# Layer norm with a residual: groups of two rows, whole 2 MB loads to the end, and fifteen tiny reads on the lowest DMA engines

## The chip, the cores and the metric

The kernel runs on one core of a Trainium2 chip. The metric is the time on the device in microseconds (us), a median over several executions. All executions used here were at a granted clock of 1.0. The profiled execution has a *span* of its own, about 2 us shorter than its measured time; times of day inside an execution count from the start of that span. ACT, DVE and POOL are the scalar, vector and GpSimd engines; the sync queue (SPq) computes nothing here, it issues DMAs. A *landing* is the semaphore update with which one DMA engine reports that its share of a DMA is done.

## The reference

```python
# x, residual: (16, 1024, 512) float32; gamma = 1, beta = 0, eps = 1e-5
z = x + residual
mean = np.mean(z, axis=-1, keepdims=True)
var = np.var(z, axis=-1, keepdims=True)
return gamma * (z - mean) / np.sqrt(var + eps) + beta
```

There are 16,384 rows of 512 numbers. Each of the 128 partitions takes 128 of them, so "a row" below is one row in every partition: 128 x 512 numbers, 256 KB. Two inputs are read and one output is written: 67.11 MB in, 33.55 MB out. Nothing can be left out of that.

## The kernel before

```python
X_CHUNKS = [8] * 15 + [4, 4]          # rows for each load of x
R_CHUNKS = [8] * 15 + [4, 4]          # ... of the residual
OUT_CHUNKS = [16] * 7 + [8, 4, 4]     # ... for each store
GROUP = 4                             # rows for each step of the computation
Z_ROWS = 64                           # ring of x; the result is written in place
R_ROWS = 32                           # ring of the residual
STORE_LAG = 40
...
def add(g):                           # POOL: one instruction a group
    nc.gpsimd.tensor_tensor(out=z, in0=z, in1=part(rbuf, R_ROWS, j0, n), op=ALU.add)

def statistics(g):                    # ACT
    for k in range(n):                # minus the mean of each row
        nc.scalar.activation(out=junk, in_=zrow(j0 + k), func=ACT.Identity,
                             scale=-inv_d, accum_out=nm[:, k : k + 1])
    for k in range(n):                # sum of squares of each row
        nc.scalar.activation(out=junk, in_=zrow(j0 + k), func=ACT.Square,
                             bias=nm[:, k : k + 1], accum_out=ssq[:, k : k + 1])
    nc.scalar.activation(out=std[:, :n], in_=ssq[:, :n], func=ACT.Sqrt,
                         bias=eps_t[:, 0:1], scale=inv_d)      # one a group
# DVE: affine1 (z + nm) * gamma, row by row; reciprocal of std, one a group;
#      affine2 z * rstd + beta, row by row
...
for lo, n in spans(X_CHUNKS):         # everything is issued from the one sync queue
    asked = lo + n
    load_x(lo, n)
    while loads_r and loads_r[0][0] + loads_r[0][1] <= asked:
        while added < loads_r[0][0] + loads_r[0][1] - R_ROWS:
            added, done = next(steps) # add, statistics, affine1, affine2 of a group
        load_r(*loads_r.pop(0))
    ...
    store_due()                       # stores of all rows up to asked - STORE_LAG
```

A load of x waits until the store of the rows that lay in the same place of the ring has landed. When the last load has been issued, 48 rows (12 MB) are left whose stores are not yet issued.

## Time and profile before

| | before |
|---|---|
| time, median | 243.29 us (243.09 to 243.51) |
| span of the profiled execution | 241.3 us |
| busy: ACT, DVE, POOL | 180.1, 178.5, 144.3 us |
| moved by DMA | 100.67 MB |
| last store issued | 225.3 us |

First the head of the profile page: the busy time of each engine; then the DMA engines' busy share in tenths and GB/s, in 40 slices of 6 us; then the DMA queues.

```profile
span 241.3 us, 1109 instructions
## 1 busy us (share of the span) xinstructions
PE 4.1 (2%) x4; PEld 1.0 (0%) x4; DVE 178.5 (74%) x290; ACT 180.1 (75%) x546; POOL 144.3 (60%) x36
...
DMA  7999999999999999999999999999999999999992
GB/s 261 434 435 434 434 430 418 421 425 432 432 470 436 391 426 421 429 434 426 430 434 437 430 424 429 429 451 410 425 426 432 475 387 418 462 434 432 413 410 117
...
## 3 DMA queue, kind: packets, MB, share of 16 engines
q1 hardware_dynamic: 6336, 100.67, 97.9%
q14 instruction: 9, 0.07, 0.1%
...
```

DMA is at nine tenths or more from the second slice to the second last. No compute engine is busy for more than 75% of the span. Queue q1 carries the kernel's loads and stores; q14 carries nine packets of kind "instruction".

The stretches of the span, with the DMA share and GB/s at the end of each line:

```profile
...
core 0: us, PE busy (x) PEld busy (x) DVE busy (x) ACT busy (x) POOL busy (x), PEclk, DMA share, GB/s
13.00:82.00 69.00, 0.00 (x0) 0.00 (x0) 60.69 (x99) 64.14 (x196) 63.05 (x14) 1.00 1.01 429
82.00:205.00 123.00, 0.00 (x0) 0.00 (x0) 99.82 (x162) 99.95 (x305) 71.98 (x16) 1.00 1.00 429
205.00:225.00 20.00, 0.00 (x0) 0.00 (x0) 17.83 (x29) 14.55 (x45) 9.05 (x2) 1.00 1.03 440
225.00:235.00 10.00, 0.00 (x0) 0.00 (x0) 0.00 (x0) 0.00 (x0) 0.00 (x0) 1.00 0.96 411
235.00:241.30 6.30, 0.00 (x0) 0.00 (x0) 0.00 (x0) 0.00 (x0) 0.00 (x0) 1.00 0.31 133
...
```

(DMA shares of 1.01 and 1.03 show that a short stretch is good to a few per cent only.) 429 GB/s is all there is: in the packet records of the trace a 16 KB packet takes 0.611 us, so 16 engines together move at most 16 x 16,384 B / 0.611 us = 429 GB/s. 100.67 MB take 234.7 us at that rate. Averaged over the 16 engines, the records show 2.0 us without a packet of the kernel's queue in the first 10 us (none starts before 1.7) and about 0.2 us in all the time from 10 to 230 us; that is what the nine packets of q14 take (9 x 0.309 us / 16).

What is lost beside the start is lost at the end. A DMA of 128 partitions is split over 16 engines, and the trace holds the moment at which each engine's share has landed. For the last store (us from the start of the span, sorted):

```
before: 236.83 236.88 236.91 236.96 236.97 236.98 236.99 237.07 237.12 237.13
        237.17 237.24 237.40 238.03 | 240.04 240.15
```

(The prediction below has these times 0.04 us later: it counted them from a slightly different start.) Two engines land about 3 us after the median of the 16. At 30 us they were not late. How they fall behind shows when their landing is set against the median of the 16 for one DMA after the other, beside the starts of q14's 8 KB packets:

```
before, the latest two of 16, us behind the median
landing near:   32    37    52    57    71    82    111   115   140   174   206   218   237
second latest: 0.11  0.11  0.10  0.58  0.56  0.79  0.98  1.47  1.71  2.24  2.18  2.92  2.95
latest:        0.11  0.60  0.59  0.89  1.08  0.83  1.11  1.98  1.98  2.56  2.52  3.03  3.05
8 KB packets of q14 at: 33.0, 52.6, 77.8, 115.0, 134.6, 169.2, 195.0, 217.4, 218.2
```

After nearly every packet of the instruction queue (not after that at 195.0) one of the two is 0.3 to 0.7 us later. A 16 KB packet that started at 33.3 us, as the first such packet ended, took 0.986 us instead of 0.611; that both ran on one engine is inferred, since the records don't name the engine of a packet.

Groups of instructions of the profile page that the change touches (busy us, mean ns of one | idle before them):

```profile
...
L120 POOL TENSOR_TENSOR zbuf<-zbuf,rbuf 128x2048 f32<-128x2048 f32 x32 | 144.1, 4526 | 70.6 <-DMA rbuf<-in_residual_dram 69.6
...
L148 ACT ACTIVATE std<-ssq,eps_t 128x4 f32<-128x4 f32 x32 | 8.5, 267 | 1.0
L173 DVE RECIPROCAL rstd<-std 128x4 f32<-128x4 f32 x32 | 5.6, 175 | 0.0
...
```

What the sync queue waited for (us in total, times, longest), and its last instructions. L84 issues the loads of x, L87 those of the residual, L90 the stores. The last line says that the fifth store from the end was issued at 181.26 and that the last one was over 44.08 us later, at 225.34.

```profile
...
engine line waited for: us in total, times, longest us
SPq L84 <- DMA out_dram<-zbuf: 112.2, 4, 29.9
...
```

```profile
...
176.36 0.33 SPq L87 DMA_DIRECT2D rbuf<-in_residual_dram  x1
181.26 44.08 SPq L90 DMA_DIRECT2D out_dram<-zbuf  x5
```

### The profile page before, as it was taken

What the parts mean: (1) busy time and instruction counts of PE and PEld (TensorE: products, weight loads), DVE (VectorE), ACT (ScalarE), POOL (GpSimd) and SP (SyncE); (2) the same over time, 40 slices, a digit from 0 to 9 for tenths busy, and PEclk for the clock granted to TensorE, in tenths of its full rate; (3) what the DMA queues carried; (4) which work ended last, traced back from release to release, by engine and by line L of the source; (5) the groups of instructions that cost most, each with busy time, mean ns of one, the idle gap of its engine ahead of it and who ended that gap; (6) DMA issues with size and microseconds to landing.
All of it is one profiled execution on the core that took longest, in us unless ns stands there. A gap on an engine that the chain in (4) does not pass through costs nothing.

```text
span 241.3 us, 1109 instructions
## 1 busy us (share of the span) xinstructions
PE 4.1 (2%) x4; PEld 1.0 (0%) x4; DVE 178.5 (74%) x290; ACT 180.1 (75%) x546; POOL 144.3 (60%) x36
## 2 busy tenths in 40 slices
PE   3300000000000000000000000000000000000000
PEld 0000000000000000000000000000000000000000
DVE  0005999999999999899934999359991699969200
ACT  2009999999999999999709997099961999697000
POOL 0088988989889507894078940889209891860000
DMA  7999999999999999999999999999999999999992
GB/s 261 434 435 434 434 430 418 421 425 432 432 470 436 391 426 421 429 434 426 430 434 437 430 424 429 429 451 410 425 426 432 475 387 418 462 434 432 413 410 117
DMA packets 6349, 100.74 MB, mean 417 GB/s; under 512 B 706, under 2 KB 706, under 8 KB 708
## 3 DMA queue, kind: packets, MB, share of 16 engines
q1 hardware_dynamic: 6336, 100.67, 97.9%
q14 instruction: 9, 0.07, 0.1%
q10 hardware_dynamic: 4, 0.00, 0.0%
HBM read 67.11 MB, written 33.55 MB: 417 GB/s over the span
## 4 chain that ended last, share of the span: by engine, by line
DMA 62%; ACT 16%; DVE 6%; POOL 6%; SPq 1%; issue 1%; DVEq 0%; POOLq 0%
DMA rbuf<-in_residual_dram 34%; DMA out_dram<-zbuf 28%; ACT junk L131 9%; ACT junk L140 7%; POOL zbuf L120 6%; DVE zbuf L175 3%; DVE zbuf L161 3%; SPq L84 1%; ACT std L148 0%; SPq L87 0%; SPq L90 0%; DVEq L261 0%; DVE rstd L173 0%; POOLq L120 0%; DVEq L161 0%
## 5 line engine op out<-in xcount | busy, mean ns | idle before, releaser
L120 POOL TENSOR_TENSOR zbuf<-zbuf,rbuf 128x2048 f32<-128x2048 f32 x32 | 144.1, 4526 | 70.6 <-DMA rbuf<-in_residual_dram 69.6
L161 DVE SCALAR_TENSOR_TENSOR zbuf<-zbuf,nm,gamma_t 128x512 f32<-128x512 f32 x128 | 89.5, 746 | 44.4 <-issue 22.5
L131 ACT ACTIVATE junk<-zbuf 128x512 f32<-128x512 f32 x128 | 74.2, 580 | 38.9 <-POOL zbuf L120 38.9
L175 DVE SCALAR_TENSOR_TENSOR zbuf<-zbuf,rstd,beta_t 128x512 f32<-128x512 f32 x128 | 87.1, 743 | 1.2
L140 ACT ACTIVATE junk<-zbuf,nm 128x512 f32<-128x512 f32 x128 | 85.9, 671 | 0.0
L140 ACT ACTIVATION_READ_ACCUMULATOR junk<-zbuf,nm 128x1 f32 x128 | 24.0, 187 | 0.0
L131 ACT ACTIVATION_READ_ACCUMULATOR junk<-zbuf 128x1 f32 x128 | 23.9, 187 | 0.0
L148 ACT ACTIVATE std<-ssq,eps_t 128x4 f32<-128x4 f32 x32 | 8.5, 267 | 1.0
L173 DVE RECIPROCAL rstd<-std 128x4 f32<-128x4 f32 x32 | 5.6, 175 | 0.0
L186 ACT ACT_TABLE_LOAD x1 | 1.3, 1283 | 1.5 <-PEq L247 1.5
L190 PE MATMUL beta_t<-gb_row,ones 1*128 1x512 f32 x2 | 2.1, 1136 | 2.3 <-DMA gb_row<-in_beta_dram 2.3
L190 PE MATMUL gamma_t<-gb_row,ones 1*128 1x512 f32 x2 | 2.0, 1122 | 2.3 <-DMA gb_row<-in_gamma_dram 2.3
L104 DVE MEMSET ones<- 1x128 f32 x1 | 0.2, 165 | 0.8 <-PEq L247 0.8
L190 PEld LDWEIGHTS beta_t<-gb_row,ones 1*128 1x128 f32 x2 | 0.5, 308 | 3.9 <-DMA gb_row<-in_beta_dram 3.9
L190 PEld LDWEIGHTS gamma_t<-gb_row,ones 1*128 1x128 f32 x2 | 0.5, 308 | 2.2 <-issue 2.2
L247 POOL MEMSET const-float32-0.0<- 128x1 f32 x1 | 0.1, 99 | 0.2 <-issue 0.2
L186 ACT ACTIVATE warm<-eps_t 128x1 f32<-128x1 f32 x1 | 0.2, 203 | 0.0
L247 POOL MEMSET const-bfloat16-1.0<- 128x1 bf16 x1 | 0.1, 102 | 0.0
L247 POOL MEMSET const-uint8-127<- 128x1 uint8 x1 | 0.1, 102 | 0.0
L247 POOL MEMSET const-float32-1.0<- 128x1 f32 x1 | 0.1, 99 | 0.0
L106 DVE MEMSET eps_t<- 128x1 f32 x1 | 0.1, 59 | 0.0
## 6 DMA issues: line engine op xcount, KB each, us to landing
zbuf<-in_x_dram SPq DMA_DIRECT2D x15, 2048.0 KB, 29.2
rbuf<-in_residual_dram SPq DMA_DIRECT2D x15, 2048.0 KB, 29.9
out_dram<-zbuf SPq DMA_DIRECT2D x7, 4096.0 KB, 28.6
zbuf<-in_x_dram SPq DMA_DIRECT2D x2, 1024.0 KB, 32.3
rbuf<-in_residual_dram SPq DMA_DIRECT2D x2, 1024.0 KB, 32.3
out_dram<-zbuf SPq DMA_DIRECT2D x1, 2048.0 KB, 23.5
out_dram<-zbuf SPq DMA_DIRECT2D x2, 1024.0 KB, 16.7
gb_row<-in_gamma_dram ACTq DMA_DIRECT2D x1, 2.0 KB
```

Source lines behind the costliest of these rows:

```text
L84: nc.sync.dma_start(out=part(zbuf, Z_ROWS, lo, n), in_=dram(xf, lo, n))
L104: nc.vector.memset(ones, 1.0)
L120: nc.gpsimd.tensor_tensor(out=z, in0=z, in1=part(rbuf, R_ROWS, j0, n), op=ALU.add)
L131: nc.scalar.activation(out=junk, in_=zrow(j0 + k), func=ACT.Identity, scale=-inv_d, accum_out=nm[:, k : k + 1],)
L140: nc.scalar.activation(out=junk, in_=zrow(j0 + k), func=ACT.Square, bias=nm[:, k : k + 1], accum_out=ssq[:, k : k + 1],)
L148: nc.scalar.activation(out=std[:, :n], in_=ssq[:, :n], func=ACT.Sqrt, bias=eps_t[:, 0:1], scale=inv_d,)
L161: nc.vector.scalar_tensor_tensor(out=zrow(j0 + k), in0=zrow(j0 + k), scalar=nm[:, k : k + 1], in1=gamma_t, op0=ALU.add, op1=ALU.mult,)
L173: nc.vector.reciprocal(out=rstd[:, :n], in_=STD.pop(g)[:, :n])
L175: nc.vector.scalar_tensor_tensor(out=zrow(j0 + k), in0=zrow(j0 + k), scalar=rstd[:, k : k + 1], in1=beta_t, op0=ALU.mult, op1=ALU.add,)
L186: nc.scalar.activation(out=warm, in_=eps_t, func=ACT.Sqrt)
L190: nc.tensor.matmul(dest, ones, gb_row[:, k, :], start=True, stop=True)
L247: nc = _bacc.Bacc("TRN2", target_bir_lowering=False, num_devices=1)
```

## The change

The intent: smaller steps, so that work starts sooner behind a load; two DMAs fewer, each of full size; and fifteen reads of a few bytes, on 15, 14, ... 1 of the DMA engines, in the same queue. They write to a tile that nobody reads, each to its own place.

```diff
-X_CHUNKS = [8] * 15 + [4, 4]
-R_CHUNKS = [8] * 15 + [4, 4]
+X_CHUNKS = [8] * 16
+R_CHUNKS = [8] * 16
 OUT_CHUNKS = [16] * 7 + [8, 4, 4]
-GROUP = 4
+GROUP = 2
...
+    few = consts.tile([16, 16, 16], FP32)
+    probes = list(range(15, 0, -1))
+
+    def probe():
+        if probes and asked > 48:
+            k = probes.pop(0)
+            nc.sync.dma_start(out=few[:k, k, :], in_=xf[:k, :16])
+
     for lo, n in spans(X_CHUNKS):
         ...
         load_x(lo, n)
+        probe()
         while loads_r and loads_r[0][0] + loads_r[0][1] <= asked:
             ...
             load_r(*loads_r.pop(0))
+            probe()
```

## The prediction

> **What bounds the kernel now.** The DMA engines. The page counts 100.67 MB on the data queue; the stretches between 13 and 205 us carry 426 to 432 GB/s. In the trace's packet records a 16 KB packet takes 0.611 us, so 16 engines move at most 429 GB/s: 234.7 us, plus 1.8 us before the first packet: 236.5. The span is 241.3. Most of the remainder is in the landings: of the last store's 16 engines, 14 land from 236.9 to 238.1, the other two at 240.1 and 240.2. These two are with the rest at 30 us and fall back in steps. The first steps, of about 0.5 us, follow the 8 KB packets of the "instruction" queue at 33.0 and 52.6 us; there are nine such packets up to 218 us. So two engines carry the instruction fetches and end 3 us late. (The Trainium skill, "DMA: Bandwidth & Descriptors", section "Queues, rings and completion order", says each engine alternates between the queues that have work for it; this trace agrees: a 16 KB packet beside the fetch at 33.0 took 0.986 us.)
>
> Compute isn't the bound: ACT 180.1, DVE 178.5, POOL 144.3 us busy. The last store is issued at 225.3 and its data only begin to move near 234.5: 9 us of slack.
>
> **What the change does.**
> - Groups of two: 32 more square roots on ACT (267 ns: +8.5 us), 32 more reciprocals on DVE (175 ns: +5.6 us), 32 more adds on POOL of half the size. ACT then needs about 24 us for 16 rows, against 28 to 30 us of DMA in the steady part. Off the critical path.
> - Whole 2 MB loads at the end: same bytes; the last eight rows are all free to start at 210.5 instead of half at 208. Eight rows of ACT are 12.4 us, plus an add of 2.3 and DVE behind: the last store is issued near 228.5. It eats 3 of the 9 us of slack.
> - Fifteen reads of 64 B rows in the sync queue. The skill (same page, "Why a DMA increments its semaphore by 16 and not by 1") says a DMA from this queue takes the lowest-numbered k engines; this trace doesn't show it yet. Engine 0 gets 15 of them, engine 15 none. A semaphore packet took 9 ns, a 2 KB gamma packet 84 to 200 ns; I estimate 20 to 80 ns a probe and engine, 0.3 to 1.2 us on engine 0. It counts only if a late engine is low-numbered. The eight rotating DMA semaphores make each DMA wait for the one eight places before; with probes among them, stores and loads are issued up to 10 us later, but I work out at least 4 MB (9.6 us) queued at each moment, as now. No hole.
> - More instructions: one or two more fetches, about 0.4 us each on a late engine.
>
> **Sum.** 243.29 + 0.4 (fetch) + 0.1 (probes, mostly on engines with 3 us to spare) = 243.8 us; 8 in 10 within 243.0 to 245.0. Faster by over 2%: 1%; within 2%: 96%; slower: 3%.
>
> **Would show it right:** GB/s of the middle unchanged; last store issued near 228.5 with DMA full until about 236; two late engines, 3 to 4 us behind; one or two more instruction packets; the probes' landings with k engines.
>
> **Would make it wrong:** a tiny read that stalls its engine for a microsecond (15 us on engine 0); a semaphore wait that lets the DMA queue run dry; the compute tail passing 235 us.

## The result and the profile after

| | before | after |
|---|---|---|
| time, median | 243.31 us (243.09 to 243.51) | 243.26 us (243.09 to 243.51) |
| span of the profiled execution | 241.3 us | 241.5 us |
| busy: ACT, DVE, POOL | 180.1, 178.5, 144.3 us | 189.8, 185.3, 148.8 us |
| last store issued | 225.3 us | 228.2 us |
| q14 packets in the span | 9 | 10 |

The ratio is 0.9999, with a 95% interval of 0.9982 to 1.0016: the same. A ratio here is the mean time of one kernel's fast runs over that of the other's in the same rounds, so it isn't quite the ratio of the medians quoted.

The same lines of the page after:

```profile
span 241.5 us, 1302 instructions
## 1 busy us (share of the span) xinstructions
PE 4.1 (2%) x4; PEld 1.0 (0%) x4; DVE 185.3 (77%) x322; ACT 189.8 (79%) x578; POOL 148.8 (62%) x68
...
DMA  7999999999999999999999999999999999999992
GB/s 261 434 434 434 432 427 421 426 419 434 432 449 434 404 429 426 434 425 422 434 430 437 434 426 430 429 442 418 432 421 422 470 400 430 470 434 434 399 410 109
...
## 3 DMA queue, kind: packets, MB, share of 16 engines
q1 hardware_dynamic: 6288, 100.67, 97.9%
q14 instruction: 10, 0.08, 0.1%
...
```

All three compute engines work longer (ACT by 9.7 us, DVE by 6.8, POOL by 4.5). The DMA row is the same, digit for digit, and q14 has one packet more inside the span.

```profile
...
core 0: us, PE busy (x) PEld busy (x) DVE busy (x) ACT busy (x) POOL busy (x), PEclk, DMA share, GB/s
13.00:82.00 69.00, 0.00 (x0) 0.00 (x0) 62.72 (x109) 65.82 (x202) 64.68 (x28) 1.00 1.01 429
82.00:205.00 123.00, 0.00 (x0) 0.00 (x0) 105.93 (x184) 107.74 (x332) 74.64 (x33) 1.00 1.01 430
205.00:225.00 20.00, 0.00 (x0) 0.00 (x0) 13.70 (x25) 14.03 (x44) 9.26 (x4) 1.00 1.01 435
225.00:235.00 10.00, 0.00 (x0) 0.00 (x0) 2.77 (x5) 0.75 (x3) 0.00 (x0) 1.00 0.97 414
235.00:241.50 6.50, 0.00 (x0) 0.00 (x0) 0.00 (x0) 0.00 (x0) 0.00 (x0) 1.00 0.31 130
...
```

The middle moves 429 to 430 GB/s as before, and the last two stretches are the same within 3 GB/s.

```profile
...
L120 POOL TENSOR_TENSOR zbuf<-zbuf,rbuf 128x1024 f32<-128x1024 f32 x64 | 148.6, 2355 | 71.7 <-DMA rbuf<-in_residual_dram 69.9
...
L148 ACT ACTIVATE std<-ssq,eps_t 128x2 f32<-128x2 f32 x64 | 17.0, 266 | 2.1
L173 DVE RECIPROCAL rstd<-std 128x2 f32<-128x2 f32 x64 | 10.5, 165 | 0.0
...
```

The square roots and reciprocals have doubled in number and nearly in total time, because 267 and 266 ns for one square root (175 and 165 for one reciprocal) hardly depend on whether it covers 4 columns or 2. The adds cost little more in all: 64 of 2.355 us instead of 32 of 4.526.

The sync queue:

```profile
...
engine line waited for: us in total, times, longest us
SPq L84 <- DMA out_dram<-zbuf: 62.7, 4, 18.8
...
SPq L226 <- DMA zbuf<-in_x_dram: 17.5, 4, 4.6
...
SPq L226 <- DMA rbuf<-in_residual_dram: 13.1, 4, 4.6
...
```

```profile
...
173.67 0.42 SPq L87 DMA_DIRECT2D rbuf<-in_residual_dram  x1
176.75 51.45 SPq L90 DMA_DIRECT2D out_dram<-zbuf  x5
```

Here one sees something that no data dependency explains. A tiny read (L226) needs nothing and nobody needs it, yet it waited for loads to land, up to 4.6 us. The landings come on eight semaphores that are used in turn, and a DMA is issued only when the one eight places before it has landed (the read issued at 152.33 us waited for a load whose last share landed at 152.31). That moves waiting from one line to another: "L84 <- DMA out_dram" fell from 112.2 to 62.7 us, in return for the waits on L226 and others. It costs nothing as long as enough is queued. The records still show about 0.2 us without a packet from 10 to 230 us.

The last store was issued at 176.75 + 51.45 = 228.2 us. Its landings:

```
after:  236.78 236.78 236.79 236.81 236.83 236.83 236.90 236.91 236.93 236.95
        237.06 237.07 237.51 239.25 | 240.11 240.33
```

The first landing is where it was, within 0.05 us. The latest is 0.18 us later, and a third engine has moved from 238.03 to 239.25.

**Which engines are late.** The tiny reads can tell. The Trainium skill ("DMA: Bandwidth & Descriptors", section "Why a DMA increments its semaphore by 16 and not by 1") says that a DMA from this queue with k shares runs on the lowest-numbered k engines, and that the sequencer itself adds the missing 16 - k at once. The trace agrees on the count: the read with k = 1 has one landing at 152.74, 0.4 us after its issue at 152.33, and one more at 174.07. The four smallest, with the landings of the whole load just ahead of each for comparison:

```
        landings of the tiny read           the load ahead of it: first, then its latest four
k = 4   149.74 150.21 151.88 152.48         149.31  150.03 150.31 151.69 152.31
k = 3   154.65 155.10 157.41                154.20  154.92 155.20 156.61 157.22
k = 2   159.60 162.29                       159.10  159.83 160.09 161.47 162.11
k = 1   174.07                              173.63  174.37 174.85 176.02 176.66
```

On each engine the tiny read lands 0.18 us after the load ahead of it, as the last column shows best (152.48 after 152.31, 157.41 after 157.22, 162.29 after 162.11). With k = 1 that leads to 173.89, which isn't among the latest four: engine 0 isn't late. With k = 2 the second landing goes with the latest of the load: engine 1 is the latest. k = 3 adds one at 155.10, which goes with 154.92 (engine 2), and k = 4 adds one at 151.88, which goes with 151.69: engine 3 is the other late one. So the two late engines are numbers 1 and 3, counted from 0, if the skill's rule of the lowest-numbered engines holds. They carry 14 and 12 of the fifteen tiny reads.

### The profile page after: what moved, and what is told of

The parts are those of the page before. It is cut to its first block, busy times and chain, and to the rows that moved or that the text cites. A ratio compares the mean times of both kernels' runs of the same rounds, so it can differ in the third digit from the quotient of the medians.

```text
span 241.5 us, 1302 instructions
## 1 busy us (share of the span) xinstructions
PE 4.1 (2%) x4; PEld 1.0 (0%) x4; DVE 185.3 (77%) x322; ACT 189.8 (79%) x578; POOL 148.8 (62%) x68
## 4 chain that ended last, share of the span: by engine, by line
DMA 82%; POOL 5%; DVE 5%; issue 1%; SPq 1%; DVEq 0%; POOLq 0%
DMA zbuf<-in_x_dram 39%; DMA rbuf<-in_residual_dram 33%; DMA out_dram<-zbuf 10%; POOL zbuf L120 5%; DVE zbuf L161 2%; DVE zbuf L175 2%; SPq L84 0%; SPq L90 0%; DVEq L272 0%; SPq L87 0%; DVE rstd L173 0%; POOLq L120 0%; DVEq L161 0%
## 5 line engine op out<-in xcount | busy, mean ns | idle before, releaser
L120 POOL TENSOR_TENSOR zbuf<-zbuf,rbuf 128x1024 f32<-128x1024 f32 x64 | 148.6, 2355 | 71.7 <-DMA rbuf<-in_residual_dram 69.9
L175 DVE SCALAR_TENSOR_TENSOR zbuf<-zbuf,rstd,beta_t 128x512 f32<-128x512 f32 x128 | 90.0, 745 | 2.3
L148 ACT ACTIVATE std<-ssq,eps_t 128x2 f32<-128x2 f32 x64 | 17.0, 266 | 2.1
L173 DVE RECIPROCAL rstd<-std 128x2 f32<-128x2 f32 x64 | 10.5, 165 | 0.0
```

Source lines behind the costliest of these rows:

```text
L173: nc.vector.reciprocal(out=rstd[:, :n], in_=STD.pop(g)[:, :n])
L175: nc.vector.scalar_tensor_tensor(out=zrow(j0 + k), in0=zrow(j0 + k), scalar=rstd[:, k : k + 1], in1=beta_t, op0=ALU.mult, op1=ALU.add,)
```

## The experiments

Twelve kernels ran; those that go together were run on the same chip with the kernel before. The theory: the 16 DMA engines are the bound, two of them end late because they also fetch instructions, and none of the three parts touches that by more than a few tenths of a microsecond. The rivals: the parts have costs and gains that cancel; or the equality has another reason than slack. All results are correct unless said otherwise.

### Each part alone

`probes_only`: the kernel before plus the tiny reads. 

> The kernel before plus the fifteen tiny reads, nothing else. My theory (the 16 DMA engines are the bound and no part of the change touches the two late ones by more than a few tenths): 243.1 to 243.8 us, ratio to before 0.999 to 1.003; each 64 B packet about 11 ns, DMA never empty. Rival (the parts have real costs and gains that cancel in the sum): this part alone costs at least 1 us, 244.3 or more.

Measured: 243.12 us, ratio 0.9998 (0.9986 to 1.0011). 120 packets of 64 B, each of 11 ns, and 10 instruction packets. The last store's latest landing is at 240.48, 0.33 us later than before.

The tenth instruction packet comes with the tiny reads. It starts at 185.7 us here and at 202.6 us in the changed kernel; the other nine start within 1.2 us of the nine of the kernel before and of `group2_only` (the next run), where the tenth starts 0.3 us after the end of the span. After it a *third* engine is late: at the last store 1.87 us behind the median here and 2.33 in the changed kernel, 0.84 to 1.06 in the three kernels without tiny reads (before, `group2_only`, `tail8_only`). So the one more fetch seems to be of the sync queue's own instructions (no record names the stream of a packet), and it falls on an engine with time to spare.

`group2_only`:

```diff
-GROUP = 4
+GROUP = 2
```

> Groups of two alone. My theory: 243.1 to 243.9 us, at most one more instruction fetch; ACT about 9.5 us and DVE about 6.5 us busier, all off the critical path. Rival (parts cancel): at least 1 us away from before, in either direction (slower through the extra instructions, or faster through the shorter tail).

Measured: 243.17 us, ratio 0.9999 (0.9985 to 1.0012); 9 instruction packets. The last store is issued at 223.2 us, 2.1 us sooner than before, and nothing comes of it.

`tail8_only`:

```diff
-X_CHUNKS = [8] * 15 + [4, 4]
-R_CHUNKS = [8] * 15 + [4, 4]
+X_CHUNKS = [8] * 16
+R_CHUNKS = [8] * 16
```

> The whole 2 MB loads to the end alone, groups of four. My theory: 243.0 to 243.7 us; the last store is issued about 3 to 6 us later than before (228 to 231 us instead of 225.3) and still before its turn in the DMA queue near 234.5. Rival (parts cancel; the longer tail costs its 3 us and the smaller groups won it back): 245 us or more.

Measured: 242.93 us, just under the range expected, ratio 0.9989 (0.9976 to 1.0002). The last store is issued at 229.9 us, 4.6 us later than before.

What follows: nothing cancels. Each part alone is within 0.25% of before, and the three intervals rule out the rival's 1 us (0.4%).

### How much slack the end has

`group8_tail8`: whole loads to the end and groups of eight, to make the end as slow as possible.

```diff
-X_CHUNKS = [8] * 15 + [4, 4]
-R_CHUNKS = [8] * 15 + [4, 4]
+X_CHUNKS = [8] * 16
+R_CHUNKS = [8] * 16
-GROUP = 4
+GROUP = 8
```

> Whole loads to the end with groups of eight, to use up the slack of the tail. My theory (the tail has about 9 us of slack in the kernel before, so a last store issued later than about 235 us shows): last store issued at 237 to 240 us, time 245 to 248 us, and DMA below 9 tenths in the last two or three slices. Rival (the tail doesn't matter at this size, the DMA total alone sets the time): within 0.5 us of before.

Measured: 243.23 us, ratio 1.0002 (0.9989 to 1.0015). The mechanism came as expected and the time didn't. The last store was issued at 237 us, as the sync queue of this run shows:

```profile
...
173.00 0.38 SPq L87 DMA_DIRECT2D rbuf<-in_residual_dram  x1
177.58 59.37 SPq L90 DMA_DIRECT2D out_dram<-zbuf  x5
```

Its 16 landings lie between 240.35 and 240.53 us: all engines together, and only 0.2 to 0.5 us after the latest two of before (240.04, 240.15). So the expectation used the wrong deadline. The queue of the *fast* engines is empty near 236 us, and there the last store must be waiting if the fast engines aren't to idle. But the kernel ends with the *late* engines. A last store of 1 MB lands 3.6 us after its issue here (240.53 - 236.95), so it delays the end only if it is issued later than about 240.15 - 3.6 = 236.6 us (an estimate from these two traces). The slack of the kernel before was thus about 11.3 us, not 9, and this run just used it up: its profiled execution, the slowest of its five, is 0.4 us past it, and the ratio shows none of that.

`pool512` was made for the instruction fetches (below), but bears on the end as well: its memsets delay the last groups.

```diff
+    idle_t = consts.tile([P, 1], FP32)
...
         nc.gpsimd.tensor_tensor(out=z, in0=z, in1=..., op=ALU.add)
+        for _ in range(16):
+            nc.gpsimd.memset(idle_t, 0.0)      # 128 x 1, used by nobody
```

> The kernel before with sixteen one-element memsets on POOL after each add, 512 instructions more, off the critical path. My theory (the late engines are late because they fetch the instruction streams[...]): four more instruction packets; if POOL's stream is fetched by one of the two late engines, that one ends 1.2 to 2.5 us later and the time is 244.3 to 246 us; if by another engine, that engine ends 1.2 to 2.5 us later and the time stays within 0.4 us. Rival (lateness has nothing to do with instructions): no engine's last landing moves by more than 0.4 us against the kernel before.

Measured: 247.14 us, ratio 1.016 (1.0146 to 1.0173), above all that was expected. POOL's last instructions of this run:

```profile
...
226.48 4.52 POOL L121 TENSOR_TENSOR zbuf<-zbuf,rbuf 128x2048 f32<-128x2048 f32 x1
230.94 2.44 POOL L125 MEMSET idle_t<- 128x1 f32 x16
```

Sixteen memsets took 2.4 us, not the 1.6 us that I had reckoned from the 0.1 us of one memset in the page before, so the last add is at 226.5 us and the last store is issued at 240.4 us. It lands at 243.79 to 243.96, all engines together, 3.5 us after its issue. That is the deadline seen from its other side: issued 3.8 us past 236.6 us, its last landing is 3.8 us later than before. As a measure of what the fetches cost in time, this run failed; what it says of lateness comes below.

### Are the tiny reads cheap, or only hidden?

`long37_k1` reads 37 pieces of 64 B in each of the fifteen places, all on the lowest engine; `long37_k4` does the same on each of the lowest four.

```diff
-    few = consts.tile([16, 16, 16], FP32)
+    few = consts.tile([1, 4, 37, 16], FP32)            # long37_k4: [4, 4, 37, 16]
...
-            k = probes.pop(0)
-            nc.sync.dma_start(out=few[:k, k, :], in_=xf[:k, :16])
+            s = probes.pop(0) % 4
+            nc.sync.dma_start(
+                out=few[:, s, :, :],
+                in_=xf[: 1 * 37, :16].rearrange("(a n) d -> a n d", a=1),   # 4 and a=4
+            )
```

> The fifteen places with one read each of 37 pieces of 64 B on one engine, the lowest: 555 packets of 11 ns are 6.1 us of that engine. It has about 3 us to spare against the two late ones. My theory: the time grows by what exceeds the spare time, 2 to 4 us, so 245 to 247.5 us. Rival (a busy engine anywhere delays the sum by its whole time or not at all): 249 us or more, or 243.

Measured: 245.36 us, ratio 1.0106 (1.0071 to 1.0141). Of the last store's landings one is at 242.46, the next at 240.29 and 239.94. Engine 0 was 0.1 us behind the median near 174 us in the changed kernel (by the landing of k = 1) and the latest engine is 5.6 us behind it here: 540 packets more cost it about 5.4 us, some 10 ns each, and 2 us of that reach the end.

> The same 37 pieces on each of the lowest four engines, among which the landings of the tiny reads put the two late ones. My theory: the late ones have no spare time, so the whole 6 us shows: 248.5 to 250.5 us, about 3 us above the run with one engine. Rival (the late engines aren't among the lowest four): the same time as the run with one engine, 245 to 247.5 us.

Measured: 250.54 us, ratio 1.03 (1.0285 to 1.0316). Four landings are at 246.1 to 247.6, the other twelve between 239.9 and 241.1.

What follows: on an engine with time to spare 5.4 us of load cost 2 us. With four engines loaded the time grows by 7.3 us, but only part of that tells of the late engines. The other twelve engines came about 3.5 us later too: 149 packets of 16 KB took over 0.7 us in place of 15 (after the first 10 us), and the time above the normal length, summed over all packets and divided by 16, grew by 3.4 us; why, I didn't separate. Against the median, two of the four are 7.0 and 7.2 us behind and two 5.7 and 6.1, where engine 0 alone was 5.6. So 1.6 us of the 5.2 us between the two runs go with late engines among the four, instead of the 3 us expected. The time is not the rival's 245 to 247.5 us, but the slow packets alone would lift it past that; that numbers 1 and 3 are the late ones rests on the landings above more than on this run. For the change itself: a 64 B packet and its semaphore packet are 11 and 9 ns, so 15 of them are about 0.3 us. They are both cheap and, on engine 0, hidden.

### Does the queue run dry?

`many4` and `many8` issue four and eight tiny reads, on one engine, in each of the fifteen places.

```diff
-    few = consts.tile([16, 16, 16], FP32)
+    few = consts.tile([1, 15 * 4, 16], FP32)                          # many8: 15 * 8
...
             k = probes.pop(0)
-            nc.sync.dma_start(out=few[:k, k, :], in_=xf[:k, :16])
+            for i in range(4):                                        # many8: 8
+                nc.sync.dma_start(out=few[:1, (k - 1) * 4 + i, :], in_=xf[:1, :16])
```

> Eight tiny reads at each of the fifteen places, 120 in all. My theory: now eight small DMAs stand between two big ones, the window of eight holds none of the big ones behind, and the DMA queue runs dry at each place for about 1 to 2.5 us: 265 to 285 us, DMA at 7 or 8 tenths between 60 and 170 us. Rival (small DMAs cost a fixed amount each): about twice the excess of the run with four, so under 2 us if that is under 1.

Measured: 284.55 us, ratio 1.1698 (1.1678 to 1.1717). The page of this run, with its slices of 7.1 us:

```profile
span 282.7 us, 1404 instructions
...
DMA  7999999995799777797777796767996999999997
GB/s 295 427 429 440 411 443 421 429 431 208 336 408 371 262 274 277 303 372 297 297 298 283 311 396 233 292 267 297 445 338 261 440 371 446 415 461 422 427 422 301
...
```

From 60 to 220 us DMA falls to seven and eight tenths, and the records show 2 to 4 us without a packet in most of the tens of microseconds there. Eight semaphores in turn and eight small DMAs between two large ones: each large one must be issued while nothing large is queued behind the last. 120 tiny reads cost 41 us, though their packets are under 0.02 us each. The holes sum to 32.7 us from 10 to 230 us; packets longer than normal add another 11 us (the excess over the changed kernel, summed over all packets and divided by 16). Some 3 us come back, because the 16 engines end together here, within 0.7 us.

> The changed kernel with four tiny reads (one engine, 64 B) at each of the fifteen places, 60 in all. My theory: the DMA semaphores go round in eights, a DMA is issued only when the one eight places before has landed; with four small ones between two big ones there is still at least one 2 MB transfer in the queue when the next is issued, so no hole: within 0.7 us of before, 243 to 244 us. Rival (each small DMA costs the queue something of its own, whatever the depth): grows by 45 more of it, several us.

Measured: 246.05 us, ratio 1.0112 (1.0096 to 1.0127). This was a miss, for the theory and for its rival. There is no hole: the records show at most 0.06 us without a packet in any 10 us from 10 to 230 us. Yet it is 2.8 us slower, and a fixed cost for each read (2.8 us for 45 more) would make only 6.5 us of the 41 us at eight. What the trace shows instead is 117 packets of 16 KB that took over 0.7 us, in bursts near 111, 125, 150, 155 and 189 us on many engines at once, against 15 in the changed kernel. Summed over all packets and divided by 16, the time above the normal length grew by 2.35 us, most of the 2.8. Why they are slow when fewer DMAs can be in flight stays open.

### What makes two engines late

`act_few` and `both_few` give wrong results. In `act_few`, ACT does one Identity and one Square for a group of four rows instead of four of each; in `both_few`, DVE also does one instruction a group in each affine step. In both, the square root and the reciprocal of a group cover one column instead of four, and the scratch pools `junkp` and `stdp` have one and two buffers instead of three.

```diff
-        for k in range(n):
-            nc.scalar.activation(out=junk, in_=zrow(j0 + k), ..., accum_out=nm[:, k : k + 1])
+        nc.scalar.activation(out=junk[:, : n * D], in_=z, ..., accum_out=nm[:, 0:1])
 # Square likewise
...
# both_few besides:
-        for k in range(n):
-            nc.vector.scalar_tensor_tensor(out=zrow(j0 + k), ..., in1=gamma_t, ...)
+        nc.vector.scalar_tensor_tensor(
+            out=z3, ..., in1=gamma_t.unsqueeze(1).to_broadcast([P, n, D]), ...)
```

> Wrong results on purpose: the kernel before with one Identity and one Square for each group of four rows instead of one for each row, 384 ACT instructions fewer. My theory (instruction fetches make the late engines late): three fetches fewer, at least one of the two late engines comes 1 us or more nearer to the rest; the time falls only if both do, so 242.0 to 243.3 us. Rival (lateness comes from HBM or from the stores): landings spread as before, 3.2 to 3.6 us, time unchanged.

Measured: 243.05 us, ratio 0.9983 (0.997 to 0.9996); 7 instruction packets. The latest engines of the last store are 2.47 and 1.34 us behind the median; before they were 3.05 and 2.95. One of the two came forward by much more than the other. Two fetches fewer, where three were expected; the profiled execution is the fastest of the five (242.32 us).

> Wrong results on purpose: the last one with one scalar_tensor_tensor for each group as well, so about 580 instructions fewer than before on ACT and DVE together. My theory: four to six instruction packets instead of nine within the span, both late engines within 1 to 1.7 us of the rest, time 241.0 to 242.2 us, ratio 0.991 to 0.996. Rival (lateness comes from HBM or the stores): spread as before and 243.2 us.

Measured: 241.27 us, ratio 0.9919 (0.9907 to 0.9932). The head of its page:

```profile
span 239.4 us, 545 instructions
...
q1 hardware_dynamic: 6336, 100.67, 98.7%
q14 instruction: 5, 0.04, 0.0%
...
```

5 instruction packets instead of 9; the latest two are 1.08 and 0.81 us behind the median; the last landing is at 238.39 instead of 240.15. The bytes, the DMAs and their order are those of before. So the two engines' lateness comes from the instructions (that it is their fetch is read from the steps after q14's packets, above), and it is on the path: taking most of it away took 1.9 us off the time. The compute engines became less busy as well, but the parts alone and `group8_tail8` show that time of that kind doesn't count here.

`pool512` supports this from the other side. At the store that lands near 227 us, before its late end matters, three engines are late: 2.90, 2.44 and 2.34 us behind the median. In the kernel before the third is at 0.88. So POOL's additional instructions made *another* engine late, as one branch of its expectation had it. That ACT's, DVE's and POOL's instructions come through three different DMA engines fits these three runs; no record names the engine of a fetch. The run had 12 instruction packets in its span, three more than before, where I had expected four.

### A version that is faster than both

`group8_only`: if instructions cost time and the size of a step doesn't, larger steps should be better. The loads stay as before, so the last groups are still of four rows.

```diff
-GROUP = 4
+GROUP = 8
```

> The kernel before with groups of eight where the loads are of eight rows; its last two loads of four stay, so its last groups are of four. Correct results. My theory of why the run with groups of eight and whole loads to the end was not slower: it had 6 instruction packets instead of 9, so its late engines were about 1 us less late, and the late last store (237 us) cost about that much. Without the long tail the gain stays: 6 or 7 instruction packets, last store issued by 227 us, landings of the last store spread over 2 to 2.8 us, time 242.0 to 242.9 us, ratio 0.994 to 0.9985. Rival (group size has no effect in either place, and the last store at 237 us was simply in time): spread 3.2 to 3.6 us and 243.2 us.

Measured: 242.34 us, ratio 0.9964 (0.9951 to 0.9978), correct. It is 0.8 us faster than before, a small gain but clear of its interval. Compare the changed kernel's 0.9999 from its own rounds.

```profile
span 240.8 us, 1004 instructions
...
q1 hardware_dynamic: 6336, 100.67, 98.1%
q14 instruction: 6, 0.05, 0.0%
...
```

Six instruction packets, as expected. But two of the four numbers of the expectation missed: the last store was issued at 229.6 us, not by 227 (harmless, by the deadline of 236.6), and its landings spread over 3.09 us, not 2 to 2.8. In the profiled execution the latest two are 2.82 and 2.48 us behind the median, only 0.23 and 0.47 less than before; the last landing is 0.36 us sooner. Single fetches in this run cost up to 1 us (one engine went from 1.84 to 2.82 us around the fetch at 151.4). So fewer fetches do mean less lateness, but not in proportion to their number. The profiled execution took 242.52 us, the slowest of the five; I can't say from one trace where the rest of the 0.8 us lies.

This also settles `group8_tail8`, as far as one trace of each allows: its own groups of eight were worth 0.4 us at the last landing (239.79 instead of 240.15), and its late last store took that back and 0.4 us more (240.53).

## Why the prediction was right

- **The bound.** DMA engines at their full rate: confirmed. 429 and 430 GB/s in the middle before and after, about 0.2 us without a packet from 10 to 230 us in both.
- **Groups of two, off the path.** ACT was predicted 8.5 us busier for the square roots, and they grew from 8.5 to 17.0 us; the reciprocals grew by 4.9 us for a predicted 5.6. Alone the groups changed nothing (0.9999).
- **The end.** The last store was predicted near 228.5 and was issued at 228.2 us. Alone, the longer loads changed nothing (0.9989, the interval includes 1). The slack was taken as 9 us; it is about 11.3 us, because the late engines set the deadline, not the fast ones. That error was on the safe side here and produced the wrong expectation for `group8_tail8`.
- **The tiny reads.** k landings each, as predicted, beside the sequencer's own. The cost on engine 0 (0.3 to 1.2 us predicted) is at the low end, about 0.3 us. The prediction said "mostly on engines with 3 us to spare"; in fact the two late engines are numbers 1 and 3 and carry 26 of the 120 shares. The reads came out harmless because they are small, not because they miss the late engines.
- **The queue.** "No hole" was right for fifteen reads and for sixty, and the limit it was worked out from, eight semaphores in turn, showed at 120. That a thinner queue may cost without a hole, 2.8 us at sixty reads, was not foreseen.
- **One or two more fetches.** One more in the span (10 packets for 9), so the number was right, but not where it comes from or falls. Groups of two alone had 9; the tenth came with the tiny reads, and it made a third engine late instead of one of the two. The 0.4 us counted for it on a late engine didn't come; the last landing is 0.18 us later in the profiled execution, about what 12 or 14 tiny reads at 20 ns take on the two late engines (an estimate).
- **The sum.** 0.5 us more was predicted, and 0.05 us less was measured, with an uncertainty of about 0.4 us. So the 0.5 us was slightly too much or lost in the noise; the times can't tell, though the traces say that the fetch's 0.4 us did not apply. The range held.

## What to carry to other kernels

When the DMA engines are full from start to end, ask of a change to the granularity of the computation what it does to the DMA engines: here the number of instructions mattered (0.8% between groups of four and few instructions) while 10 us of ACT time did not. Look at the landings of single engines, not only at the mean DMA share, since the slowest of 16 ends the kernel and sets the real deadline for the last store. And before putting small DMAs among large ones, count how many DMAs may be in flight: fifteen cost nothing measurable, 60 cost 2.8 us and 120 cost 41 us, mostly through the waits between them, not through their bytes.

## What the Trainium skill lacked or had wrong

- "DMA: Bandwidth & Descriptors", section "Queues, rings and completion order", calls queue row 14 runtime-internal and lists what it carries, without a price. In these runs an instruction packet of 8 KB makes the engine that carries it, in most cases, 0.3 to 1.0 us late for the kernel's own data, the loss falls on two or three engines only, and it set the end of the kernel by 3 us. The page "Runtime: NRT & Kernel Launch", section "Instruction fetch mechanics", has no number for it either.
- The same page, section "Latency and other measured facts", names engines 7 and 15 as usually slower, and offers a cause that is specific to its SWDGE path. Here, with all large DMAs issued from the sync queue, the late ones are 1 and 3, by the skill's own rule of the lowest-numbered k.
- The same page, section "Where 436 GB/s comes from", gives a ceiling of 435 GB/s. The packets here take 0.611 us for 16 KB, which makes 429 GB/s over 16 engines, and the middle of the span holds it: 1.4% below the ceiling, so no contradiction.
- The same page advises against many small transfers, but has no number for small packets among large ones; its time for one small packet, in section "Bandwidth", is for transfers issued from GpSimd. Here a 64 B packet took 11 ns of its engine and the semaphore packet 9 ns.
- No page says how few DMAs may be in flight from one queue of a kernel built like this one. Here, with eight semaphores in turn, the time grew by 41 us when eight tiny reads stood between the large ones.
